# Gate and up products of a transformer trunk's last feed-forward half as block products: seven half-sized products in the place of eight

## The chip, the cores and the metric

The kernel runs on one core of a Trainium2 chip. Its engines are PE (TensorE, matrix products), DVE (VectorE), ACT (ScalarE), POOL (GpSimd) and SP (SyncE, which issues the loads). Each takes its instructions in a fixed order and waits for the others by semaphores. The metric is the device time of one execution in microseconds (us), lower is better.

## The reference

Two layers on 512 latent tokens and 256 context tokens of 1024 channels, in fp32. Each layer is a feed-forward half, a mixer (a convolution module in layer 0, neighbourhood attention in layer 1) and a second feed-forward half. The change touches the last one alone, which works on the 512 latent tokens (`D = 1024`, `F = 2816`):

```
def _swiglu(h, wg, wu, wd):
    return (jax.nn.silu(h @ wg) * (h @ wu)) @ wd

def _ffn_half(s, mod, g, wg, wu, wd):
    shift, scale, gate = mod
    h = _modulate(_rmsnorm(s, g), shift, scale)
    return s + 0.5 * gate * _swiglu(h, wg, wu, wd)
...
    return _rmsnorm(x, final_g)
```

## The kernel before

Channels lie on the partitions, tokens on the free axis; 1024 channels are 8 chunks of 128. fp32 accuracy comes from splitting: every weight tile and every activation is split into a rounded part `hi` (ACT, a copy to fp32r) and a remainder `lo` (DVE, a subtraction `src - hi` of two SBUF operands), and `mm3` makes three matmuls of each product: hi x hi, hi x lo, lo x hi.

The feed-forward half (`ffn`) runs over 22 blocks of 128 hidden columns in `GROUPS` of 5, 5, 6 and 6. For a block it loads a gate and an up tile of 128 x 1024 weights (`load`, three buffers each of `raw`, `whi`, `wlo`), and for the last half of the kernel makes products for two pieces of tokens (`HALVES`: 256 and 256 + 2 columns; the two extra columns hold the products of the shift vector). A block is therefore 2 weights x 2 pieces x 8 chunks x 3 = 96 matmuls. The factor of the norm, `rb`, is applied to the products when DVE reads them out of PSUM (`by_rows`, L289); then come SiLU on ACT (L318), `tu` on DVE (L319) and the split of the hidden tile into `hidh` and `hidl` (L115, L116). After each group, `down` multiplies the group's hidden tiles with `dn` for 8 output chunks `d` and adds to `x` (L296). In the last group the two halves of the tokens (`LATS`) go one after the other, and `finish` normalises and stores the first half while the second is worked on: its column sums are L182, its factor is made by the Newton steps (L166 to L177), spread by L194, and the outputs are multiplied at L852, on POOL for the first half and on DVE for the second.

Before this half stand the attention's output products: 8 units of 24 matmuls of 512 columns (L833 to L835 evict them), and then `scaled_parts` (L225, L226) makes the half's input `h` from `x`. The tiles of `h` take over the buffers of the attention's output (tags `hhi` and `hlo`), chunk by chunk as the last unit has read them.

The order of the instructions on each engine is made by a list scheduler when the program is built; the tile pools' buffers decide what may overlap. PSUM has 8 banks: three of tag `a`, two of `b`, two of `c` and one `st`.

## Time and profile before

| what | us |
|---|---|
| median of 3 runs | 2747.91 (2747.2 to 2749.19) |
| span of the profiled execution | 2745.9 |
| PE busy in it | 2700.0 (98%) |
| DVE, ACT, POOL busy | 1673.2, 822.1, 68.1 |
| last feed-forward half: first product to the end | 2351.3 to 2745.9 |

The span runs from the first to the last instruction in the profile. The profiled execution's own time is not listed apart from its span; the timed executions are 1.3 to 3.3 us longer than that span, and 2.0 us is taken for what lies around it. Busy is the time in which an engine works on at least one instruction; PE overlaps its matmuls, so what a matmul costs is read from the distance of the starts of two that follow each other.

### The profile page before, as it was taken

How to read it: one execution, taken by the hardware profiler on the slowest of the kernel's cores; microseconds unless marked ns; L12 is line 12 of the kernel's file. 1: busy time of each engine (PE TensorE's matmuls, PEld its weight loads, DVE VectorE, ACT ScalarE, POOL GpSimd, SP SyncE). 2: the span in 40 equal slices, each digit the busy share in tenths (PEclk: the TensorE clock that was granted, in tenths of full speed). 3: DMA queues.
4: the chain of work that ended last, by engine and by line, in shares of the span. 5: the costliest groups of instructions: out<-in, count | busy, mean ns of one | idle time of the engine just before them, and what ended most of it. 6: DMA issues, size and time to landing. Idle time of an engine off the chain costs nothing.

```text
span 2745.9 us, 41215 instructions
## 1 busy us (share of the span) xinstructions
PE 2700.0 (98%) x16948; PEld 2353.4 (86%) x16948; DVE 1673.2 (61%) x3048; ACT 822.1 (30%) x1306; POOL 68.1 (2%) x124
## 2 busy tenths in 40 slices
PE   8999999999989999999999999999999999999997
PEld 4888888888869888888888888888888888999997
DVE  5999533357998999833363433433478576544446
ACT  4212221241236212121242221212346455422224
POOL 0000000011020100000000000000000000000001
PEclk9999999999999999999999999999999999999999
DMA  8565212122435565412121212121242121233223
GB/s 297 163 211 175 88 55 71 56 71 78 127 78 178 168 195 177 158 54 70 58 72 50 75 50 67 61 69 61 80 121 62 58 73 46 74 105 95 88 99 112
DMA packets 95101, 277.73 MB, mean 101 GB/s; under 512 B 11329, under 2 KB 25793, under 8 KB 94657
## 3 DMA queue, kind: packets, MB, share of 16 engines
q1 hardware_dynamic: 94336, 273.52, 31.4%
q8 instruction: 133, 2.18, 0.3%
q0 software_dynamic: 576, 1.57, 0.2%
q14 instruction: 56, 0.45, 0.1%
HBM read 269.09 MB, written 4.38 MB: 100 GB/s over the span
## 4 chain that ended last, share of the span: by engine, by line
PE 93%; DVE 3%; ACT 1%; issue 1%; DMA 1%; POOL 0%; SPq 0%; DVEq 0%; POOLq 0%; ACTq 0%
PE a L125 12%; PE a L123 12%; PE a L124 11%; PE c L123 9%; PE c L125 9%; PE c L124 9%; PE b L125 8%; PE b L124 8%; PE b L123 8%; PE st L793 2%; PE b L784 1%; DVE y L514 1%; PE c L532 1%; PE a L759 1%; PE a L760 1%
## 5 line engine op out<-in xcount | busy, mean ns | idle before, releaser
L110 ACT ACTIVATE whi<-raw 128x1024 fp32r<-128x1024 f32 (+2 forms) x376 | 360.0, 960 | 1437.8 <-PE c L124 1046.0
L111 DVE TENSOR_TENSOR wlo<-raw,whi 128x1024 fp32r<-128x1024 f32 (+2 forms) x376 | 411.8, 1098 | 100.1 <-ACT whi L110 98.1
L125 PE MATMUL a<-hhi,wlo 128*128 128x512 f32 (+2 forms) x1264 | 442.2, 350 | 0.4 <-DVE wlo L111 0.4
L124 PE MATMUL a<-hlo,whi 128*128 128x512 f32 (+2 forms) x1264 | 440.3, 348 | 0.0
L123 PE MATMUL a<-hhi,whi 128*128 128x512 f32 (+2 forms) x1264 | 440.3, 349 | 0.0
L123 PE MATMUL c<-hhi,whi 128*128 128x258 f32 (+2 forms) x1456 | 428.6, 295 | 4.3 <-ACT hhi L115 2.1
L125 PE MATMUL c<-hhi,wlo 128*128 128x258 f32 (+2 forms) x1456 | 429.2, 295 | 0.0
L124 PE MATMUL c<-hlo,whi 128*128 128x258 f32 (+2 forms) x1456 | 427.1, 294 | 0.5 <-DVE hlo L116 0.5
L375 DVE SCALAR_TENSOR_TENSOR junk<-mraw,sbc 128x1024 f32<-128x1024 f32 x256 | 312.7, 1221 | 3.8 <-ACT sbc L360 2.0
L123 PEld LDWEIGHTS c<-hhi,whi 128*128 128x128 f32 x1456 | 275.7, 190 | 15.6 <-ACT hhi L115 2.7
L123 PE MATMUL b<-hhi,whi 128*128 128x512 f32 (+2 forms) x800 | 280.3, 350 | 6.0 <-ACT hhi L225 3.4
L124 PEld LDWEIGHTS c<-hlo,whi 128*128 128x128 f32 x1456 | 276.7, 190 | 10.8 <-DVE hlo L116 1.3
L125 PE MATMUL b<-hhi,wlo 128*128 128x512 f32 (+2 forms) x800 | 280.9, 351 | 0.5 <-DVE wlo L111 0.5
L125 PEld LDWEIGHTS c<-hhi,wlo 128*128 128x128 f32 x1456 | 275.1, 189 | 7.1 <-issue 1.0
L124 PE MATMUL b<-hlo,whi 128*128 128x512 f32 (+2 forms) x800 | 280.1, 350 | 0.5 <-DVE hlo L226 0.5
L125 PEld LDWEIGHTS a<-hhi,wlo 128*128 128x128 f32 x1264 | 237.8, 188 | 34.0 <-issue 1.1
L124 PEld LDWEIGHTS a<-hlo,whi 128*128 128x128 f32 x1264 | 238.1, 188 | 32.9 <-issue 0.2
L123 PEld LDWEIGHTS a<-hhi,whi 128*128 128x128 f32 x1264 | 238.0, 188 | 31.3 <-issue 0.8
L123 PEld LDWEIGHTS b<-hhi,whi 128*128 128x128 f32 x800 | 151.0, 189 | 29.6 <-ACT hhi L225 3.6
L124 PEld LDWEIGHTS b<-hlo,whi 128*128 128x128 f32 x800 | 151.0, 189 | 22.8 <-DVE hlo L226 1.0
L125 PEld LDWEIGHTS b<-hhi,wlo 128*128 128x128 f32 x800 | 150.9, 189 | 22.2 <-DVE wlo L111 1.0
L124 PE MATMUL a<-hidl,whi 128*128 128x512 f32 (+1 forms) x431 | 162.7, 377 | 0.0
(202 smaller groups left out, 4169.8 us busy)
## 6 DMA issues: line engine op xcount, KB each, us to landing
raw<-in_gu SPq DMA_DIRECT2D x176, 512.0 KB
mraw<-in_modv SPq DMA_DIRECT2D x128, 512.0 KB
raw<-in_dn SPq DMA_DIRECT2D x80, 384.0 KB
raw<-in_dn SPq DMA_DIRECT2D x64, 320.0 KB
raw<-in_pw SPq DMA_DIRECT2D x24, 512.0 KB
us<-v SPq DMA_DIRECT2D x64, 142.0 KB
mraw<-in_modp SPq DMA_DIRECT2D x16, 512.0 KB
raw<-in_wqk SPq DMA_DIRECT2D x16, 512.0 KB
```

What stands on the lines that cost most here:

```text
L110: nc.scalar.activation(hi[:, :cols], raw[:, :cols], AF.Copy)
L111: nc.vector.tensor_tensor(lo[:, :cols], raw[:, :cols], hi[:, :cols].bitcast(F32), ALU.subtract)
L123: nc.tensor.matmul(po, lhsT=whi[:, s], rhs=ah[:, o:o + n], start=first and i == 0, stop=False)
L124: nc.tensor.matmul(po, lhsT=whi[:, s], rhs=al[:, o:o + n], start=False, stop=False)
L125: nc.tensor.matmul(po, lhsT=wlo[:, s], rhs=ah[:, o:o + n], start=False, stop=last and i == k - 1)
L375: nc.vector.scalar_tensor_tensor(junk, raw, 1.0, sbc[:, s, :], ALU.mult, ALU.mult, accum_out=m[:, s, c:c + 1])
L514: nc.vector.scalar_tensor_tensor(yo, u[:, k:k + n], w, yo, ALU.mult, ALU.add)
L532: nc.tensor.matmul(po[ST * g:ST * g + ST, e:e + PIECE], lhsT=dg[:, 4 * m + g], rhs=t[:, g, 4 * m:4 * m + PIECE], start=m == 0, stop=m == 7)
L759: nc.tensor.matmul(so, lhsT=qq[:, qsl], rhs=kk[:, ks], start=True, stop=False)
L760: nc.tensor.matmul(so, lhsT=ql[:, qsl], rhs=kk[:, ks], start=False, stop=True)
L784: nc.tensor.transpose(pt[:, i * P:(i + 1) * P], p[:, i * P:(i + 1) * P], ident)
L793: nc.tensor.matmul(po[64 * a:64 * a + 64, :P], lhsT=v[:, c0:c0 + 64], rhs=PT[a][:, i * P:(i + 1) * P], start=i == 0, stop=i == 3)
```

## The change

For the last half, the gate and the up weights are taken in pairs of blocks: 256 hidden columns by 1024 channels. With the channels cut into two halves (even and odd chunks), the tokens into two halves of 256 (each with a shift column pair, so 258 columns), and the hidden columns into two blocks, a pair is a 2 x 2 by 2 x 2 block product. `s_unit` makes it of seven products of half the depth (4 chunks, 12 matmuls of 258 columns) instead of eight: 84 matmuls for a unit (gate or up of a pair) in the place of 96. Products 1 to 4 and 5 to 7 are named after the operands that they need:

* `s_prepare` makes sums and differences of the activations once (`tt`, four DVE subtractions for each of 4 steps `j`), and splits all seven operands into the buffers that held `h`; `slots[:4]` hold operands 1, 2, 3, `slots[4:]` operands 5, 6, 7, and `t4` operand 4. The scaling by the modulation is done into `sg` tiles (two buffers) beforehand.
* `s_weights` makes sums and differences of the weights for every unit on POOL: four instructions of 128 x 512, two SBUF operands each, into `s12` and `s34` (one buffer each). Four tiles are split for a unit, of 1024, 1024, 1024 and 512 columns: the raw tile for products 1 and 2, `s12` for 6 and 5, `s34` for 7 and 3, and half of the second raw tile for product 4. They go through the same three `whi` and `wlo` buffers.
* Products 1, 6, 7 and 4 accumulate in one PSUM bank (`a`), 5 and 3 in another (`c`), 2 in a third (`b`). Intermediate states are copied out by ACT (`kept`, L396; L414), and DVE adds them to the banks (L403, L410, L412). The norm's factor is applied afterwards, on SBUF tiles (L967, L974).
* The groups are `PAIRS` of 3, 3, 3 and 2 pairs, that is 6, 6, 6 and 4 blocks, so `down` has 432 matmuls of 512 columns and 192 of 256 instead of 384 and 288.

The rest of the program, up to the last output product of the attention, stands in the same order as before. The diff, cut to its core:

```diff
-TB = T + 2
+SB = 258
+TB = 3 * SB
...
+PAIRS = (3, 3, 3, 2)
...
+    def s_weights(src, pool):
+        raws = []
+        for i in range(2):
+            raw = main.tile([P, 1024], F32, tag="raw", name="raw", bufs=3)
+            nc.sync.dma_start(raw, src[i])
+            raws.append(raw)
+        q = [raws[0][:, :512], raws[0][:, 512:], raws[1][:, 512:], raws[1][:, :512]]
+        s12 = pool.tile([P, 1024], F32, tag="s12", name="s12", bufs=1)
+        s34 = pool.tile([P, 1024], F32, tag="s34", name="s34", bufs=1)
+        s1, s2, s3, s4 = s12[:, 512:], s12[:, :512], s34[:, :512], s34[:, 512:]
+        sums = ((s1, q[2], q[3], ALU.add), (s2, s1, q[0], ALU.subtract), (s3, q[0], q[2], ALU.subtract),
+                (s4, q[1], s2, ALU.subtract))
+        made = {}
+        for t, names in ((raws[0], (1, 2)), (s12, (6, 5)), (s34, (7, 3)), (raws[1], (4,))):
+            if t is s12:
+                for o, a, b, op in sums:
+                    nc.gpsimd.tensor_tensor(o, a, b, op)
+            n = 512 * len(names)
+            hi = main.tile([P, 1024], F32R, tag="whi", name="whi", bufs=3)
+            lo = main.tile([P, 1024], F32R, tag="wlo", name="wlo", bufs=3)
+            split(hi[:, :n], lo[:, :n], t[:, :n])
+            for i, name in enumerate(names):
+                made[name] = (hi, lo, 512 * i)
+        return made
+    def s_unit(src, hs, pool, row):
+        w = row.shape[3]
+        made = s_weights(src, pool)
+        def product(name, p, first):
+            hi, lo, o = made[name]
+            for j in range(4):
+                k = slice(o + j * P, o + j * P + P)
+                ah, al = hs[name][j]
+                for i, (a, b) in enumerate(((hi, ah), (hi, al), (lo, ah))):
+                    nc.tensor.matmul(p, lhsT=a[:, k], rhs=b, start=first and j == 0 and i == 0,
+                                     stop=j == 3 and i == 2, skip_group_check=True)
+        def kept(p):
+            t = pool.tile([P, w], F32, tag="kept", name="kept", bufs=4)
+            nc.scalar.activation(t, p, AF.Copy)
+            return t
+        x, y = bank("a")[:, :w], bank("b")[:, :w]
+        product(1, x, True)
+        a = kept(x)
+        product(2, y, True)
+        nc.vector.tensor_tensor(row[:, 0, 0], y, a, ALU.add)
+        product(6, x, False)
+        b = kept(x)
+        z = bank("c")[:, :w]
+        product(5, z, True)
+        d = kept(z)
+        product(7, x, False)
+        nc.vector.tensor_tensor(row[:, 1, 1], x, d, ALU.add)
+        product(3, z, False)
+        nc.vector.tensor_tensor(row[:, 0, 1], z, b, ALU.add)
+        product(4, x, False)
+        nc.scalar.activation(row[:, 1, 0], x, AF.Copy)
+    def s_prepare(j, hs, sx, tt, A, B):
+        for r in range(2):
+            c = 2 * j + r
+            nc.scalar.activation(sx[:, r, :, :256], xl[c].rearrange("p (b n) -> p b n", b=2), AF.Identity,
+                                 scale=A[:, 0, c:c + 1])
+            nc.gpsimd.tensor_copy(sx[:, r, :, 256:], B[:, 0, c:c + 1].rearrange("p (a b) -> p a b", a=1).broadcast_to([P, 2, 2]))
+        nc.vector.tensor_tensor(tt[:, 0], sx[:, 0, 1], sx[:, 0, 0], ALU.subtract)
+        nc.vector.tensor_tensor(tt[:, 1], sx[:, 1, 1], tt[:, 0], ALU.subtract)
+        nc.vector.tensor_tensor(tt[:, 2], sx[:, 1, 1], sx[:, 0, 1], ALU.subtract)
+        nc.vector.tensor_tensor(tt[:, 3], sx[:, 1, 0], tt[:, 1], ALU.subtract)
+        for names, src in (((1,), sx[:, 0, :1]), ((2, 3), sx[:, 1]), ((5, 6, 7), tt[:, :3]), ((4,), tt[:, 3:])):
+            to = hs[names][j]
+            split(to[0], to[1], src)
...
-        h = new_h()
...
-        for d in range(NC):
-            scaled_parts(h, d, (LAT,), derv[1, 7], mods[1, 6])
+    with tc.tile_pool(name="ffn3", bufs=1) as hid:
+        slots = new_h()
+        t4 = [hid.tile([P, 4, SB], F32R, name=f"t4{i}") for i in range(2)]
+        hs = {}
+        for names, of in (((1, 2, 3), slots[:4]), ((5, 6, 7), slots[4:])):
+            for i, n in enumerate(names):
+                hs[n] = [tuple(t[:, i * SB:(i + 1) * SB] for t in of[j]) for j in range(4)]
+        hs[4] = [tuple(t[:, j] for t in t4) for j in range(4)]
+        spans = {}
+        for names in ((1,), (2, 3), (5, 6, 7)):
+            of = slots[:4] if names[0] < 5 else slots[4:]
+            o = SB if names[0] == 2 else 0
+            spans[names] = [tuple(t[:, o:o + len(names) * SB].rearrange("p (a n) -> p a n", n=SB) for t in of[j])
+                            for j in range(4)]
+        spans[(4,)] = [tuple(t[:, j:j + 1] for t in t4) for j in range(4)]
+        def rows(tag):
+            return hid.tile([P, 2, 2, SB], F32, tag=tag, name=tag, bufs=2)
+        for j in range(4):
+            s_prepare(j, spans, rows("sg"), rows("tu").rearrange("p a b n -> p (a b) n"), derv[1, 7], mods[1, 6])
         rms_rows((LAT,), True)
...
-        ffn(3, h, hid, HALVES, (1, 8), nothing, finish)
+        rows_rb = rb[:, :TL].rearrange("p (b n) -> p b n", b=2)
+        pair = 0
+        for gi, gn in enumerate(PAIRS):
+            last = gi == len(PAIRS) - 1
+            hids = []
+            f0 = 2 * pair
+            for _ in range(gn):
+                sg, tu = rows("sg"), rows("tu")
+                s_unit(gs[pair, 0], hs, hid, sg)
+                for r in range(2):
+                    so = sg[:, r, :, :256]
+                    nc.vector.tensor_tensor(so, so, rows_rb, ALU.mult)
+                    nc.scalar.activation(so, so, AF.Silu, bias=sg[:, r, 0, 256:257])
+                s_unit(gs[pair, 1], hs, hid, tu)
+                for r in range(2):
+                    to = tu[:, r, :, :256]
+                    hh = hid.tile([P, TL], F32R, tag="hidh", name="hidh", bufs=7)
+                    hl = hid.tile([P, TL], F32R, tag="hidl", name="hidl", bufs=7)
+                    nc.vector.tensor_tensor(to, to, rows_rb, ALU.mult)
+                    nc.vector.scalar_tensor_tensor(to, to, tu[:, r, 0, 256:257], sg[:, r, :, :256], ALU.add, ALU.mult)
+                    split(hh.rearrange("p (b n) -> p b n", b=2), hl.rearrange("p (b n) -> p b n", b=2), to)
+                    hids.append((hh, hl))
+                pair += 1
+            for st in LATS if last else (LAT,):
+                for d in range(NC):
+                    n = 2 * gn * P
+                    w = load(dn[3, d, :, f0 * P:f0 * P + n], n)
+                    down(d, w, hids, st, derv[1, 8], last)
+                if last:
+                    finish(st)
...
+def _quarters(w):
+    k, m = w.shape
+    t = w.reshape(k // 256, 2, P, m // 256, 2, P).transpose(3, 4, 2, 1, 0, 5)
+    t = np.stack([t[:, 0], t[:, 1, :, ::-1]], axis=1)
+    return t.reshape(m // 256, 2, P, k)```

Three places of the order on the engines, in which the names are `raw` loaded weights, `s12` and `s34` the POOL's sums, `whi` and `wlo` split weights, `sg` the gate's and `tu` the up's tile of a pair, `kept` a copied PSUM state, and `a`, `b`, `c` PSUM banks. The first place is the middle of a group. On DVE, before, a block's instructions stand like this:

```order
L289 TENSOR_TENSOR sg_22106<-a_22006,rb_84 128x256
L289 TENSOR_TENSOR tu_22109<-b_22031,rb_84 128x256
L289 TENSOR_TENSOR sg_22106<-a_22056,rb_84 128x256
L282 COPY bcol_22112<-a_22056 128x2
L111 TENSOR_TENSOR wlo_22129<-raw_22126,whi_22128 128x1024
L289 TENSOR_TENSOR tu_22109<-a_22081,rb_84 128x256
L282 COPY bcol_22114<-a_22081 128x2
L319 SCALAR_TENSOR_TENSOR tu_22109<-tu_22109,bcol_22114,sg_22106 128x512
L111 TENSOR_TENSOR wlo_22251<-raw_22248,whi_22250 128x1024
L116 TENSOR_TENSOR hidl_22005<-tu_22109,hidh_22004 128x512
```

On DVE in the changed kernel, a gate unit's stretch there, in which the hidden tiles of the pair before are finished (`tu_21939`, `hidl`) among the weight splits of this unit and the first of the next one (`raw_22331`):

```order
L403 TENSOR_TENSOR sg_22202<-b_22231,kept_22244 128x258
L118 TENSOR_TENSOR wlo_22223<-s34_22209,whi_22222 128x1024
L118 TENSOR_TENSOR hidl_22191<-tu_21939,hidh_22190 128x512
L974 TENSOR_TENSOR tu_21939<-tu_21939,rb_84 128x2x256
L118 TENSOR_TENSOR wlo_22227<-raw_22206,whi_22226 128x512
L975 SCALAR_TENSOR_TENSOR tu_21939<-tu_21939,sg_21938 128x2x256
L118 TENSOR_TENSOR wlo_22338<-raw_22331,whi_22337 128x1024
L410 TENSOR_TENSOR sg_22202<-a_22230,kept_22286 128x258
L118 TENSOR_TENSOR hidl_22197<-tu_21939,hidh_22196 128x512
L412 TENSOR_TENSOR sg_22202<-c_22273,kept_22271 128x258
L118 TENSOR_TENSOR wlo_22346<-s12_22335,whi_22345 128x1024
L967 TENSOR_TENSOR sg_22202<-sg_22202,rb_84 128x2x256
```

A unit has seven to nine DVE instructions with two SBUF operands here, and three that read PSUM; before, a block of two weights had four such with two SBUF operands. The second place is the same stretch on ACT, in the up unit that follows:

```order
L396 ACTIVATE kept_22371<-a_22357 128x258
L117 ACTIVATE whi_22349<-s34_22336 128x1024
L968 ACTIVATE sg_22202<-sg_22202 128x2x256
L117 ACTIVATE whi_22353<-raw_22333 128x512
L414 ACTIVATE sg_22202<-a_22230 128x258
L396 ACTIVATE kept_22398<-a_22357 128x258
L968 ACTIVATE sg_22202<-sg_22202 128x2x256
L117 ACTIVATE whi_22474<-raw_22468 128x1024
```

The first split of the next unit, `whi_22474`, stands behind the second SiLU of the gate (the second L968), which needs DVE's L967 on what L414 copied. The third place is the head of a group on PE, where product 6 of a unit ends (`whi_21954`), the first matmuls of the next unit's products 1 and 2 follow (`whi_22073`), and then product 7 begins (`whi_21958`):

```order
L391 MATMUL a_21966<-hhi7_20840,whi_21954 128x258
L391 MATMUL a_21966<-hlo7_20841,whi_21954 128x258
L391 MATMUL a_21966<-hhi7_20840,wlo_21955 128x258
L391 MATMUL a_22093<-hhi0_20826,whi_22073 128x258
L391 MATMUL a_22093<-hlo0_20827,whi_22073 128x258
L391 MATMUL b_22094<-hhi0_20826,whi_22073 128x258
L391 MATMUL b_22094<-hlo0_20827,whi_22073 128x258
L391 MATMUL a_21966<-hhi4_20834,whi_21958 128x258
```

`whi_22073` takes over the buffer of `whi_21954`. In the other units product 7 stands ahead of these four matmuls. On PE the order in a unit, from then on, is: 2 matmuls of product 5, product 6, the other 10 of product 5, product 7, two each of the next unit's products 1 and 2, product 3, the other ten each of the next 1 and 2, and product 4 at their end or 4 matmuls ahead of it.

## Rows read from the trace of the kernel before

**Rows 1.** The page's busy times, share of the span and instructions of each engine.

```profile
PE 2700.0 (98%) x16948; PEld 2353.4 (86%) x16948; DVE 1673.2 (61%) x3048; ACT 822.1 (30%) x1306; POOL 68.1 (2%) x124
```

**Rows 2.** Windows (us from the span's start) of the last half.

```profile
core 0: us, PE busy (x) PEld busy (x) DVE busy (x) ACT busy (x) POOL busy (x), PEclk, DMA share, GB/s
2351.00:2400.00 49.00, 46.76 (x386) 45.66 (x384) 27.05 (x67) 18.90 (x32) 0.00 (x0) 1.00 0.22 68
```

**Rows 3.** Groups by form, 2340 to 2746 us: busy us, mean ns, idle before.

```profile
L124 PE MATMUL a<-hlo,whi 128*128 128x258 f32 x216 | 61.1, 283 | 0.0
...
L111 DVE TENSOR_TENSOR wlo<-raw,whi 128x1024 fp32r<-128x1024 f32 x44 | 53.8, 1223 | 14.9 <-ACT whi L110 13.9
...
L319 DVE SCALAR_TENSOR_TENSOR tu<-tu,bcol,sg 128x512 f32<-128x512 f32 x22 | 16.5, 752 | 2.9 <-ACT whi L110 0.5 <-ACT sg L318 0.4
L318 ACT ACTIVATE sg<-sg,bcol 128x512 f32<-128x512 f32 x22 | 15.6, 709 | 0.3 <-DVE bcol L282 0.3
...
L116 DVE TENSOR_TENSOR hidl<-tu,hidh 128x512 fp32r<-128x512 f32 x22 | 15.1, 686 | 0.0
...
L289 DVE TENSOR_TENSOR tu<-a,rb 128x256 f32<-128x256 f32 x27 | 11.4, 424 | 36.9 <-PE a L125 36.9
```

**Rows 4.** Timeline of PE into the last half: start, duration, instruction, idle before.

```profile
2345.76 0.40 PE L123 MATMUL a<-hhi,whi 128*128 128x512 f32 x1
...
2351.10 0.40 PE L125 MATMUL a<-hhi,wlo 128*128 128x512 f32 x1
...
2359.31 0.29 PE L124 MATMUL a<-hlo,whi 128*128 128x258 f32 x1
...
2361.12 0.28 PE L124 MATMUL a<-hlo,whi 128*128 128x258 f32 x1
...
2364.03 0.28 PE L123 MATMUL a<-hhi,whi 128*128 128x256 f32 x1
...
2366.38 0.28 PE L125 MATMUL a<-hhi,wlo 128*128 128x256 f32 x1
2367.76 1.10 PE L194 MATMUL st<-t,ones 128*128 128x512 f32 x2 [1.09 <-DVE t L188]
2370.00 0.39 PE L123 MATMUL b<-hhi,whi 128*128 128x256 f32 x1 [1.15 <-DVE sg L289]
```

**Rows 5.** Timeline of ACT and DVE, same stretch.

```profile
2354.41 0.76 ACT L833 ACTIVATE t<-a,dv,mod 128x512 f32<-128x512 f32 x1
...
2363.29 2.01 ACT L110 ACTIVATE whi<-raw 128x1024 fp32r<-128x1024 f32 x2 [5.40 <-PE b L124]
...
2365.59 1.22 DVE L111 TENSOR_TENSOR wlo<-raw,whi 128x1024 fp32r<-128x1024 f32 x1
2366.73 0.16 DVE L173 SCALAR_TENSOR_TENSOR nwt<-nwt 128x4 f32<-128x4 f32 x1
```

**Rows 6.** Timeline of DVE and POOL where both work.

```profile
40.74 0.80 POOL L209 TENSOR_TENSOR acc<-acc,t 128x256 f32<-128x256 f32 x1
40.87 0.95 DVE L226 SCALAR_TENSOR_TENSOR hlo<-xc,dv,hhi 128x256 fp32r<-128x256 f32 x1
...
2724.69 0.42 DVE L209 TENSOR_TENSOR acc<-acc,t 128x256 f32<-128x256 f32 x1
...
2725.99 5.11 POOL L852 TENSOR_TENSOR out<-out,rb 128x1024 f32<-128x1024 f32 x2 [3.65 <-ACT rb L218]
2726.42 2.44 DVE L209 TENSOR_TENSOR acc<-acc,t 128x256 f32<-128x256 f32 x1
2728.78 0.47 DVE L296 SCALAR_TENSOR_TENSOR x<-b,dv,x 128x256 f32<-128x256 f32 x1
```

**Rows 7.** One POOL line's instructions: ns min/median/max.

```profile
L520 POOL TENSOR_TENSOR dg<-eye,parts x12: 1906/2024/8445, 596.8 to 799.0; 128x1024 f32<-128x1024 f32 x12
```

**Rows 8.** Timeline of PE at the kernel's end.

```profile
2730.00 0.28 PE L125 MATMUL b<-hidh,wlo 128*128 128x256 f32 x1
2734.16 1.02 PE L182 MATMUL st<-ones,acc 128*128 128x1 f32 x4 [3.88 <-DVE acc L209]
```

More of the change, by code (lines that the diff above doesn't have):

```diff
@@ L55, in tile_trunk @@
 @with_exitstack
-def tile_trunk(ctx: ExitStack, tc, xin, cb, cs, par, modp, modv, gu, dn, pw1, pw2, wqk, wv, wo, bv, rpb, out):
+def tile_trunk(ctx: ExitStack, tc, xin, cb, cs, par, modp, modv, gu, gs, dn, pw1, pw2, wqk, wv, wo, bv, rpb, out):
     nc = tc.nc
@@ L835, in tile_trunk @@
             square_in(d, LAT)
-        for d in range(NC):
-            scaled_parts(h, d, (LAT,), derv[1, 7], mods[1, 6])
+    with tc.tile_pool(name="ffn3", bufs=1) as hid:
[17 more added lines that the diff above has]
+            s_prepare(j, spans, rows("sg"), rows("tu").rearrange("p a b n -> p (a b) n"), derv[1, 7], mods[1, 6])
         rms_rows((LAT,), True)
-    with tc.tile_pool(name="ffn3", bufs=1) as hid:
         def finish(st):
@@ L905, in _layout @@
     gate, up, down = (i[k].reshape(4, *i[k].shape[2:]) for k in ("ffn_w_gate", "ffn_w_up", "ffn_w_down"))
-    g["gu"] = np.stack([np.stack([_tiles(gate[k]), _tiles(up[k])], axis=1) for k in range(4)])
+    g["gu"] = np.stack([np.stack([_tiles(gate[k]), _tiles(up[k])], axis=1) for k in range(3)])
+    g["gs"] = np.stack([_quarters(gate[3]), _quarters(up[3])], axis=1)
     g["dn"] = np.stack([_tiles(down[k]) for k in range(4)])
@@ L918, in _layout @@
     return {k: np.ascontiguousarray(v) for k, v in g.items()}
-_INS = ["xin", "cb", "cs", "par", "modp", "modv", "gu", "dn", "pw1", "pw2", "wqk", "wv", "wo", "bv", "rpb"]
+_INS = ["xin", "cb", "cs", "par", "modp", "modv", "gu", "gs", "dn", "pw1", "pw2", "wqk", "wv", "wo", "bv", "rpb"]
 def kernel(**inputs):
```

1 line of the change is left out of this document (added).

## The prediction

> **What bounds the kernel now.** The page comes first: PE is busy for 98% of the span [rows 1], so the question is what PE waits for and what one of its matmuls costs. The windows show the last half alone: PE at the full clock (PEclk 1.00, that is 2.4 GHz) and busy but for 2.2 us of the first 49, DVE about half busy, POOL idle [rows 2]. The timeline gives the cost of a matmul as the distance of two starts: 512 columns 5.34 us over 23 steps, 0.2322; 258 columns 1.81 over 15, 0.1207; 256 columns 2.35 over 20, 0.1175 [rows 4]. The recorded 283 ns of such a matmul [rows 3] overlap. So PE time in this half goes by columns, and fewer matmuls are worth their full price as long as the other engines deliver. The reader should also see one hole: PE stands still from the start at 2366.38 to 2370.00, about 3.6 us, while the norm's factor is made and DVE can't free the PSUM banks without it [rows 4].
>
> **What is removed on PE.** Gate and up before: 22 blocks x 96, half of 256 and half of 258 columns, 1056 x 0.1175 + 1056 x 0.1207 = 251.5 us. After: 22 units x 84 = 1848 x 0.1207 = 223.1. The down products: 48 more of 512 columns (+11.1) and 96 fewer of 256 (-11.3). Together **-28.6 us**. If 258-column slices that begin at other offsets cost more, this shrinks; no row shows that, and I add nothing for it.
>
> **What is added, engine by engine.** DVE instructions overlap by some 0.08 us: a split of 1024 columns is recorded with 1.22 and followed by the next start after 1.14 [rows 5]. With 0.08 off the means [rows 3], a split of 512 or a product with `rb` is 0.61, the line like L319 0.66, and an addition from PSUM 0.34 (nearest row: L289, 424 ns). Per pair DVE then has 6 x 1.14 + 2 x 0.61 of weight splits, 6 x 0.34, and 4 x 0.61 + 2 x 0.66 + 2 x 0.61 on the tiles: about 15.1 us, of which 13.0 have two SBUF operands. PE needs 168 x 0.1207 = 20.3 us for a pair. DVE alone would do.
>
> POOL's eight sums a pair decide. No row has one of 128 x 512; L209 with 256 columns takes 0.80 and L520 with 1024 takes 1.9 at least [rows 6, 7], so one takes about 1.2 us. What they do to DVE is in [rows 6]: L209 on DVE, 0.42 us elsewhere, took 2.44 while POOL's L852 (2.56 each) ran, 2.02 longer; L226 with 256 columns took 0.95 beside a POOL instruction of 256, against the 0.47 of L296, which has the same form and size, 0.48 longer. L296 reads PSUM, and took its 0.47 although POOL ran beside it. So a POOL instruction holds up DVE instructions with two SBUF operands for most of its length: 0.48 at 256, 2.02 at 1024, hence about 0.97 us at 512. The Trainium skill has this as a rule (SBUF — State Buffer, section "SBUF: two separate sides"): VectorE instructions with two SBUF inputs and GpSimd instructions share one port pair, which the first to start locks for its whole instruction. The rows agree on the lock, but the hold that they show is shorter than the instruction.
>
> So 8 x 0.97 = 7.8 us of POOL and 13.0 of DVE exclude each other: 20.8 of 20.3 us. That isn't hopeless over a group, since the last unit of a group has no sums beside it and the first has some made during the down products. But the splits have dates. I follow one unit; 0 is the start of its product 5.
>
> *Gate unit.* The buffer for its `s34` split is freed by product 4 of the unit before, 0.5 us before 0; ACT (1.0 us a split [rows 5]) is done at 0.55. POOL's second sum holds the port until 1.2, the low part is done at 2.3. Then in DVE's order `hidl` to 2.9, POOL's third sum to 3.9, L974 to 4.5, the fourth sum to 5.5, the split for product 4 to 6.1, L975 to 6.7, and the next unit's first low part to 7.9. PE wants it after products 5, 6, 7, four matmuls and product 3 (52 x 0.1207) at 6.3: **1.6 late**. Without the sums it would be there at 5.3, **0 late**.
>
> *Up unit.* The same split is done on ACT at 1.0 and on DVE at 2.5; the split for product 4 at 3.1, POOL's third sum 4.1, L967 4.7, then the second SiLU on ACT (0.63 after overlap) 5.3, and only then the next unit's first high part, 6.3. PE wants it at 4.35: **1.95 late**; without the sums 5.1, **0.75 late**.
>
> *Head of a group.* Product 7 stands behind matmuls that need a split whose buffer product 6 frees: one split on ACT, **1.1**.
>
> There are 11 gate and 11 up units. The 4 up units that end a group have no following unit; in the 4 gate units that begin one, two splits are made before, and I take half, 0.8. Three heads (the first group's order is another): 3.3. In full: 3.3 + 4 x 0.8 + 7 x 1.6 + 7 x 1.95 = 31.4 us. With the sums costing nothing: 3.3 + 7 x 0.75 = 8.6. POOL got the port within a DVE instruction or two nearly always (L520's median 2.0 is near its minimum of 1.9, though one took 8.4 [rows 7]), so I take a value near the upper end: **+29**.
>
> **The start.** Before, ACT and DVE scale and split chunk by chunk, and PE has work from 2351.3 on; its loss is the 3.6 us hole. After, ACT first holds one 1024-column split and the eviction of the last attention unit (at 2354.4 before [rows 5]), and steps 2 and 3 need the two `sg` buffers of steps 0 and 1. A step costs DVE 4 differences at 0.34 and 1806 columns of splits (0.34 + 0.6 + 0.87 + 0.34), 3.5 us. Adding these up in DVE's order, with the split of `s34` (1.14), the last `x` and the squares, step 3 is ready at about 2362.7. PE has products 1, 2, 5 and 6 until then (48 x 0.1207 = 5.8 us from 2351.3), so it ends them at 2363.6 instead of 2357.1: 6.5 lost. L194 now stands in PE's order among the next products and waits some 1.2 for DVE and takes 1.1; four sums of POOL in the way cost DVE about 1.5. Together 10.3, **+6.7** net; bounds +1 (steps go by PE's other work) to +11 (each of eight sums holds DVE here).
>
> **The end.** Before, PE stops at 2730.3 and its last column sums wait until 2734.16 for DVE, held up by L852 on POOL [rows 6, 8]. After, the second half of the tokens takes PE 96 x 0.1175 = 11.3 us instead of 144 x 0.1175 = 16.9, so L852 falls on the last Newton steps and multiplications instead: it moves the hold, and saves or costs up to 4. Steps of 12 matmuls (1.4 us) are about what DVE needs for theirs (0.61 + 0.39 + 0.34) and what a load allows, +1. I take **+0.5**, -3 to +4.
>
> **The sum.** -28.6 + 29 + 6.7 + 0.5 = +7.6 us on a span of 2745.9, 2753.5; with 2.0 around it **2755 us**, against a median of 2747.91. PE's clock is left at full: the rows show PEclk 1.00 over the window with the 3.6 us hole [rows 2], and the new waits are of that length or shorter.
>
> **Rivals.**
> *The sums slip in* (faster). POOL takes DVE's waits for ACT and PE, and the splits are on time; the waits are those worked out without sums. For it: DVE has 5 us a pair without work, and L296 shows that PSUM instructions go on beside POOL. Against it: in the gate unit DVE has none of those waits between 1.2 and 6.7. -28.6 + 8.6 + 6.7 + 0.5 = -12.8: 2735. It decides from the point where stalls in the units are under 16 us.
> *Half of it* (no change). POOL is sometimes held off by a chain of DVE instructions, as the 8.4 us of L520 show, and comes in at the PSUM additions: 20 us of stalls, 2746.
> *The hold is the whole instruction* (slower). If a sum keeps the port for its recorded 1.2 us instead of 0.97, two sums in each of 14 units add 14 x 2 x 0.23 = 6.4: 2762. The 0.48 beside a record of 0.80 speak against it. This is what the rule of the Trainium skill's SBUF page (same section) would give.
>
> **Chances.** About 0.2% (5.5 us) is what a measurement of this kernel can tell from no change. My forecast has 0.38, with a range of its own of 2750 to 2766; the longer hold 0.07; half 0.27; sums that slip in 0.28. So faster 0.28, no change 0.27, slower 0.45. The range must reach into the faster case's middle, and above it takes in the longer hold with the start's upper bound: 2734 to 2770.
>
> **What would show it right or wrong.** PE: 1848 matmuls with starts 0.1207 apart, and idle time of some 20 to 30 us spread over the units, ended by ACT's `whi` or DVE's `wlo`, least in the last unit of a group. A pair in the middle of a group should take about 23.8 us instead of 20.3. DVE's splits and tile products beside POOL should be 0.5 to 1 us longer than 1.22 and 0.69 in many places, its PSUM additions not. POOL's sums should take 1.2 to 2 us. If splits keep their length and pairs take 21, the sums slip in. The hole before the first SiLU should be gone, and one of 6 us should stand in the first 12. Wrong from the ground up I'd be if the 258-column matmuls keep another distance, or if PE's clock falls at the start.

## The result and the profile after

The changed kernel takes **2780.05 us** in the median of 4 executions (2774.3 to 2784.5), against 2747.84 (2747.2 to 2749.2): 1.0115 times as long, 95% interval 1.0101 to 1.0130. The prediction had the sign (slower) but not the size: 2755, range 2734 to 2770. The profiled execution, the longest of the four, has a span of 2782.7 us, 36.8 more than before.

The windows of the changed kernel answer to [rows 2]. The granted clock (PEclk) is below 1.00 in the stretches in which the units of a group run, and PE is busy for only 42 to 44 of 50 us there; where down products fill the stretch (2450 to 2500) it is as before:

```profile
core 0: us, PE busy (x) PEld busy (x) DVE busy (x) ACT busy (x) POOL busy (x), PEclk, DMA share, GB/s
2351.00:2400.00 49.00, 41.53 (x262) 37.97 (x261) 40.59 (x60) 26.62 (x44) 19.81 (x16) 0.83 0.14 44
2450.00:2500.00 50.00, 48.48 (x307) 43.04 (x306) 32.59 (x35) 19.84 (x30) 19.02 (x13) 1.00 0.31 100
2500.00:2550.00 50.00, 42.20 (x310) 40.94 (x310) 39.25 (x44) 21.99 (x37) 18.96 (x12) 0.93 0.25 76
```

From the distances of PE's matmul starts, in each trace from 2351.2 to the last down product, with 0.119 us taken for 258 columns, 0.2322 for 512 and 0.1165 for 256: distances over 0.5 us above these count as waits; the smaller excesses are parted by the granted clock at their place, 0.50 (that is 1.2 GHz) or full.

| us | before | changed | difference |
|---|---|---|---|
| work | 372.1 | 344.5 | -27.7 |
| waits | 2.9 | 39.7 | +36.8 |
| smaller excesses at half clock | 0 | 17.9 | +17.9 |
| smaller excesses at full clock | 3.4 | 10.2 | +6.8 |
| from the last down product to the end | 15.6 | 18.6 | +3.0 |
| sum | | | +36.8 |

(Before, a further 3.9 us of wait lies behind the last down product [rows 8] and is counted in the last row, in the changed kernel 6.5.) Of the 17.9 us at half clock, 5.9 fall into the first 24 us and 12.0 into the units. So the saving on PE came as forecast; waits and a slower PE took more than twice as much back. The waits of PE, by what ended them:

```profile
engine line waited for: us in total, times, longest us
PE a L391 <- DVE wlo L118: 19.5, 8, 3.6
PE a L391 <- ACT whi L117: 9.0, 9, 2.0
```

The groups of DVE instructions by form answer to [rows 3] (busy us, mean ns, idle before). Those with two SBUF operands are longer than they were, 1.45 and 1.54 us for 1.22, 1.45 for 0.69; the additions out of PSUM (L403) are not:

```profile
L118 DVE TENSOR_TENSOR wlo<-s,whi 128x1024 fp32r<-128x1024 f32 x44 | 63.8, 1449 | 9.8 <-ACT whi L117 7.0 <-PE a L391 2.5
L118 DVE TENSOR_TENSOR wlo<-raw,whi 128x1024 fp32r<-128x1024 f32 x22 | 34.0, 1544 | 9.2 <-ACT whi L117 8.7
L118 DVE TENSOR_TENSOR wlo<-raw,whi 128x512 fp32r<-128x512 f32 x22 | 31.8, 1447 | 1.4 <-ACT whi L117 1.3
...
L403 DVE TENSOR_TENSOR sg<-b,kept 128x258 f32<-128x258 f32 x11 | 4.7, 426 | 7.7 <-PE b L391 6.6 <-ACT whi L117 1.0
```

One wait in the middle of a group shows how it comes about. These are rows of the timeline, engine by engine (start, duration, instruction, idle before): the gate unit whose split of `s34` opens at 2497.68.

```profile
2497.43 0.28 PE L391 MATMUL a<-t,wlo 128*128 128x258 f32 x1
...
2497.68 1.06 ACT L117 ACTIVATE whi<-s 128x1024 fp32r<-128x1024 f32 x1 [1.69 <-PE a L391]
...
2498.78 2.37 DVE L118 TENSOR_TENSOR wlo<-s,whi 128x1024 fp32r<-128x1024 f32 x1
2501.06 1.80 DVE L118 TENSOR_TENSOR hidl<-tu,hidh 128x512 fp32r<-128x512 f32 x1
2502.78 1.80 DVE L974 TENSOR_TENSOR tu<-tu,rb 128x512 f32<-128x512 f32 x1
2504.50 1.78 DVE L118 TENSOR_TENSOR wlo<-raw,whi 128x512 fp32r<-128x512 f32 x1
2506.20 0.74 DVE L975 SCALAR_TENSOR_TENSOR tu<-tu,sg 128x512 f32<-128x512 f32 x1
2506.87 1.21 DVE L118 TENSOR_TENSOR wlo<-raw,whi 128x1024 fp32r<-128x1024 f32 x1
...
2498.74 1.31 POOL L371 TENSOR_TENSOR s<-raw 128x512 f32<-128x512 f32 x1 [5.79 <-DVE sg L403]
2500.13 2.18 POOL L371 TENSOR_TENSOR s<-s,raw 128x512 f32<-128x512 f32 x1
2502.25 1.78 POOL L371 TENSOR_TENSOR s<-raw 128x512 f32<-128x512 f32 x1
2503.99 1.74 POOL L371 TENSOR_TENSOR s<-raw,s 128x512 f32<-128x512 f32 x1
...
2504.27 0.28 PE L391 MATMUL c<-hhi,wlo 128*128 128x258 f32 x1
2508.13 0.39 PE L391 MATMUL a<-hhi,wlo 128*128 128x258 f32 x1 [3.58 <-DVE wlo L118]
```

Read it from the top. PE's last matmul of product 4 frees a weight buffer; ACT splits, then DVE runs six instructions one behind the other until 2508.08, and PE takes the last one's result at 2508.13. DVE never idles in these 9.3 us. But the first four take 1.09 to 1.15 us longer than alone (1.22, 0.68, 0.68, 0.69), and in each of them POOL works on one of its sums: POOL and DVE take turns. 4 x 1.12 = 4.5 of the 9.3 us are the time lost to POOL's sums.

Behind this wait PE runs at half clock. The windows behind it, and around the 1.73 us wait that follows at 2519.78:

```profile
2509.00:2512.00 3.00, 3.00 (x16) 3.00 (x15) 2.08 (x4) 0.39 (x1) 0.00 (x0) 0.50 0.50 175
2508.13:2513.58 5.45, 5.45 (x32) 5.45 (x33) 3.58 (x7) 2.17 (x4) 1.31 (x1) 0.69 0.42 152
2518.00:2521.00 3.00, 1.27 (x11) 1.22 (x11) 1.26 (x3) 1.94 (x3) 1.16 (x1) 1.00 0.31 127
```

The second of these windows holds 32 matmuls, up to the first one behind the next product 4. A wait of nearly the same kind, of 2.63 us, ends at 2427.90, and behind it the clock stays up: the corresponding 32 matmuls take 3.97 us instead of 5.45.

```profile
2427.90 0.39 PE L391 MATMUL a<-hhi,wlo 128*128 128x258 f32 x1 [2.63 <-DVE wlo L118]
...
2427.90:2431.87 3.97, 3.97 (x33) 3.97 (x33) 3.53 (x7) 2.21 (x4) 0.00 (x0) 1.00 0.54 171
```

The start of the half, where before the clock was 1.00 [rows 2]: rows of the windows, and of the timelines of PE, DVE and POOL.

```profile
2351.00:2362.00 11.00, 6.16 (x29) 4.28 (x28) 11.00 (x14) 8.64 (x15) 7.37 (x8) 0.84 0.00 0
2362.00:2372.00 10.00, 9.36 (x39) 8.57 (x40) 9.34 (x27) 4.23 (x9) 0.00 (x0) 0.50 0.01 2
...
2362.55 0.58 PE L391 MATMUL a<-hlo,whi 128*128 128x258 f32 x1 [3.47 <-DVE hlo L118]
...
2358.96 1.78 DVE L914 TENSOR_TENSOR x<-x,t 128x512 f32<-128x512 f32 x1
2360.67 1.50 DVE L423 TENSOR_TENSOR tu<-sg 128x258 f32<-128x258 f32 x1
...
2358.78 1.42 POOL L371 TENSOR_TENSOR s<-raw 128x512 f32<-128x512 f32 x1 [2.18 <-DVE wlo L118]
2360.15 1.73 POOL L371 TENSOR_TENSOR s<-raw,s 128x512 f32<-128x512 f32 x1
```

PE is busy for 6.2 of the first 11 us; the next 10 run at 1.2 GHz. Here too two sums stand in DVE's way: L914 takes 1.78 instead of 0.68, L423 1.50 instead of 0.42.

And the end, which answers to [rows 6, 8]: the wait before the last column sums has grown from 3.88 to 6.46, because POOL's two output multiplications meet the last additions of squares, as before [rows 6], and four of these now take 6.11 us (0.42 each alone).

```profile
2764.83 6.11 DVE L211 TENSOR_TENSOR acc<-acc,t 128x256 f32<-128x256 f32 x4
...
2765.31 4.82 POOL L951 TENSOR_TENSOR out<-out,rb 128x1024 f32<-128x1024 f32 x2 [2.85 <-ACT rb L220]
...
2770.99 1.02 PE L184 MATMUL st<-ones,acc 128*128 128x1 f32 x4 [6.46 <-DVE acc L211]
```

### The profile page after: what moved, and what is told of

Its sections match the earlier page's. It is cut to its first block, busy times and chain, and to the rows that moved or that the text cites. A ratio compares the mean times of both kernels' runs of the same rounds, so it can differ in the third digit from the quotient of the medians.

```text
span 2782.7 us, 40958 instructions
## 1 busy us (share of the span) xinstructions
PE 2700.1 (97%) x16636; PEld 2339.2 (84%) x16636; DVE 1789.1 (64%) x3078; ACT 887.8 (32%) x1438; POOL 210.2 (8%) x220
## 4 chain that ended last, share of the span: by engine, by line
PE 89%; DVE 6%; issue 1%; ACT 1%; DMA 1%; POOL 0%; SPq 0%; DVEq 0%; ACTq 0%; POOLq 0%
PE a L127 10%; PE a L125 10%; PE a L126 9%; PE c L125 9%; PE c L127 9%; PE c L126 9%; PE b L127 6%; PE b L125 6%; PE b L126 6%; PE a L391 4%; PE st L874 2%; PE c L391 1%; DVE wlo L118 1%; PE b L865 1%; PE b L391 1%
## 5 line engine op out<-in xcount | busy, mean ns | idle before, releaser
L112 ACT ACTIVATE whi<-raw 128x1024 fp32r<-128x1024 f32 (+3 forms) x332 | 311.5, 942 | 1246.2 <-PE c L126 1045.3
L125 PE MATMUL c<-hhi,whi 128*128 128x258 f32 (+2 forms) x1456 | 428.5, 295 | 4.3 <-ACT hhi L117 2.1
L113 DVE TENSOR_TENSOR wlo<-raw,whi 128x1024 fp32r<-128x1024 f32 (+3 forms) x332 | 355.5, 1073 | 89.3 <-ACT whi L112 88.2
L127 PE MATMUL a<-hhi,wlo 128*128 128x512 f32 (+1 forms) x832 | 321.0, 386 | 0.4 <-DVE wlo L113 0.4
L125 PE MATMUL a<-hhi,whi 128*128 128x512 f32 (+1 forms) x832 | 319.1, 384 | 0.0
L126 PE MATMUL a<-hlo,whi 128*128 128x512 f32 (+1 forms) x832 | 318.8, 383 | 0.0
L125 PEld LDWEIGHTS c<-hhi,whi 128*128 128x128 f32 x1456 | 275.7, 190 | 15.6 <-ACT hhi L117 2.7
L125 PE MATMUL b<-hhi,whi 128*128 128x512 f32 (+1 forms) x528 | 204.0, 386 | 4.9 <-ACT hhi L227 3.4
L127 PE MATMUL b<-hhi,wlo 128*128 128x512 f32 (+1 forms) x528 | 204.8, 388 | 0.5 <-DVE wlo L113 0.5
L126 PE MATMUL b<-hlo,whi 128*128 128x512 f32 (+1 forms) x528 | 203.6, 386 | 0.8 <-DVE hlo L228 0.8
L125 PEld LDWEIGHTS a<-hhi,whi 128*128 128x128 f32 x832 | 156.4, 188 | 31.2 <-issue 0.8
L125 PE MATMUL a<-hidh,whi 128*128 128x512 f32 (+1 forms) x432 | 165.1, 383 | 0.9 <-ACT hidh L117 0.4
L127 PE MATMUL a<-hidh,wlo 128*128 128x512 f32 (+1 forms) x432 | 164.0, 380 | 0.2 <-DVE wlo L113 0.2
L125 PE MATMUL c<-hidh,whi 128*128 128x256 f32 x528 | 149.3, 283 | 0.0
```

The source lines that it names most:

```text
L112: nc.scalar.activation(hi[:, :cols], raw[:, :cols], AF.Copy)
L113: nc.vector.tensor_tensor(lo[:, :cols], raw[:, :cols], hi[:, :cols].bitcast(F32), ALU.subtract)
L125: nc.tensor.matmul(po, lhsT=whi[:, s], rhs=ah[:, o:o + n], start=first and i == 0, stop=False)
L126: nc.tensor.matmul(po, lhsT=whi[:, s], rhs=al[:, o:o + n], start=False, stop=False)
L127: nc.tensor.matmul(po, lhsT=wlo[:, s], rhs=ah[:, o:o + n], start=False, stop=last and i == k - 1)
```

## Experiments

The theories in turn: **A**, POOL's sums hold up DVE's instructions with two SBUF operands, and that makes the waits. **B**, the added work of ACT and DVE is late by its order or amount, whoever makes the sums. **C**, loads come late. **D** and **E** came with the later runs.

One thing has to be known for all of them: the list scheduler makes the order of the engines anew for every version. The two runs without sums keep the changed kernel's order on PE, DVE and ACT, and the one with four load buffers nearly so; with the sums on DVE, with matmuls filled in place and with a tile of its own for product 4 the order changes too, and what such a run gains belongs to the edit and the new order together.

### Without the sums, and with POOL only writing

```diff
-                    nc.gpsimd.tensor_tensor(o, a, b, op)
+                    nc.gpsimd.memset(o, 0.01)
```

> The four sums of weight quarters on POOL are replaced by POOL writing a constant into the same tiles, at the same places of the order (this leaves the sums out, so the products are not the reference's). POOL stays busy, but it no longer reads two SBUF operands, and the sums no longer wait for the loads. Theory A (a POOL sum holds up DVE's instructions with two SBUF operands, about 1.1 us each, and the waits so made drop PE's clock): if a write of a constant holds nothing, PE's waits in the units fall from some 30 us to under 10, the clock stays at 1.00 outside the first 25 us, and the time is 2735 to 2745; if any POOL instruction holds DVE, it stays at 2770 or more with DVE splits still 1.4 to 1.5 us. Theory B (the order and amount of the added ACT and DVE work makes the splits late, whoever makes the sums): 2770 to 2785 with splits at 1.22 us.

The other run takes the line out and fills `s12` and `s34` once, ahead of the units.

> No sums at all: the splits of the second and third part of a unit's weights read two tiles that are filled once (this leaves the sums of the weights out, so the products are not the reference's). Theory A: as forecast without sums, 8.6 us of waits in the units, of which none is long enough to drop the clock; -28 of PE work, +9 of waits, about +12 at the start and +3 at the end: 2740 to 2748. Theory B: waits of 2.5 us and more remain in every second unit and the time is 2765 or more. Theory C (loads come late because the three load buffers are held by the sums): also fast here, but then the run with sums on DVE, which holds them as long, stays slow.

Measured: 2736.91 and **2737.17 us** (ratios 0.9956 and 0.9959). Both are theory A's, the second a little better than expected. The splits of `s` are back at their length (ns, minimum/median/maximum; the first fence is the run in which POOL writes, the second the run without sums), and the stretch of a pair in the second run is filled by PE at full clock:

```profile
L118 DVE TENSOR_TENSOR wlo<-s,whi x40: 1214/1224/1228, 2381.6 to 2680.2; 128x1024 fp32r<-128x1024 f32 x40
```

```profile
L118 DVE TENSOR_TENSOR wlo<-s,whi x40: 1214/1225/1226, 2382.5 to 2681.1; 128x1024 fp32r<-128x1024 f32 x40
...
2482.00:2502.30 20.30, 20.30 (x172) 20.30 (x171) 15.81 (x23) 12.52 (x21) 0.00 (x0) 1.00 0.31 105
```

So the sums cost 2780.05 - 2737.17 = 43 us. And it isn't POOL's being busy: POOL that writes a constant holds nothing. The Trainium skill says this (SBUF — State Buffer, section "Who interferes with whom"): a VectorE instruction with two SBUF inputs contends with a GpSimd instruction that reads SBUF, not with one that only writes it. The run in which POOL writes agrees: the splits kept 1.22 us.

Both runs have the changed kernel's order, so nothing but the sums differs. By the distances of PE's starts, the 47.8 us between the two profiled spans (2782.7 and 2734.9) are 26.4 of waits in the units (31.2 against 4.8), 12.0 of half clock there (against none), 3.9 of waits at the start, and 5.5 in small pieces. So the chain runs from the sums to the waits, and from the waits to the clock.

### The sums on DVE

```diff
-                    nc.gpsimd.tensor_tensor(o, a, b, op)
+                    nc.vector.tensor_tensor(o, a, b, op)
```

> The four sums of weight quarters of a unit run on DVE instead of POOL, all else as changed. Theory A (hold): a sum then costs DVE about 0.61 us instead of the 1.13 that the POOL sum takes from it, 2.1 us less in front of each next split, so the waits of 2.6 to 3.7 us fall to 0.5 to 1.6 and those of 0.9 to 1.9 to nothing, the clock stays up, and the time is 2745 to 2760. Theory B (amount of DVE work): DVE has 20 us of work in a pair of 20.3 us of PE, and its waits for ACT and PE come on top, so it is 2780 to 2800.

Measured: **2746.09 us**, ratio 0.9991 (0.9982 to 1.0001). A sum takes DVE 0.68 us instead of the 1.12 that it lost to POOL's. DVE has more instructions, B expected it slower, and it is 34 us faster. That B falls rests on the two runs before, which keep the order; here the order is another too.

```profile
L371 DVE TENSOR_TENSOR s<-raw x42: 680/684/695, 2348.1 to 2681.4; 128x512 f32<-128x512 f32 x42
```

### Four load buffers

In the changed kernel the load of a unit's second quarters is issued at 2494.09, when a split has freed one of three buffers, and its last packet lands at 2498.25; POOL's first sum begins at 2498.74, behind the end of DVE's L403, which its row names. So all four sums stand ahead of the next split, where the forecast had three. Is that loop the cause?

```diff
-            raw = main.tile([P, 1024], F32, tag="raw", name="raw", bufs=3)
+            raw = pool.tile([P, 1024], F32, tag="rs", name="rs", bufs=4)
```

> As changed, sums on POOL, but the quarters are loaded into four buffers of their own instead of the three that all weight loads share (to make room, the hidden rows have 6 buffers instead of 7 and the output tile one instead of two). Theory A (the hold alone): every sum still takes 1.1 us from DVE, four of them stand in front of the next unit's split, and the time stays at 2770 to 2785. Theory C (a loop through the loads: a unit's second load is issued only when the split of the unit before has freed its buffer, lands 4.1 to 4.5 us later, then four sums of 1.3 to 2.2 us and two splits, 14 us a unit): with the fourth buffer the loads are early, the loop is cut, a mid pair takes 21 to 24 us instead of 25.5 to 27.6, and the time is 2745 to 2762.

Measured: 2778.2 us. C falls as the main cause. The first sum of the unit that corresponds does start ahead of the split, at 2491.32 (split at 2493.39), and three sums are left in front of PE; its wait is still 2.31 us, and the distance of two such waits 25.3 instead of 26.4 us. New waits of 1.7 us for the first down weights of three groups take about 5 us back; whether the smaller hidden buffers cause them was not tried.

```profile
2501.32 0.39 PE L391 MATMUL a<-hhi,wlo 128*128 128x258 f32 x1 [2.31 <-DVE wlo L118]
```

With the sums on DVE the loads give nothing either:

> Sums on DVE and the quarters in four buffers of their own (hidden rows 6 buffers, output tile one). Without POOL the units show hardly any wait for weights but 1.2 us at two places a group, so the loads have little to give: 2743 to 2747. If the loads still delay the first group and the heads, 2738 to 2742.

Measured: 2746.99, as without it (2746.09).

### What half clock costs in the units

```diff
+        for i in range(fill):
+            if i == 0:
+                warm = pst()
+            nc.tensor.matmul(warm[:, :w], lhsT=hs[1][0][0][:, :P], rhs=hs[1][0][0], start=True, stop=True)
```

> As changed, with 18 matmuls of 258 columns into an unused PSUM bank ahead of each up unit but the first (2.2 us of PE work where PE now waits 2.5 to 3.7 us; their product is not used). If the waits are what drops PE's clock, the clock stays at 1.00 through these ten units, the waits shrink by the 2.2 us that the added work fills, and the kernel loses the 1.6 to 2 us of half clock that follow each of them: 16 to 20 us less than the changed kernel, 2760 to 2766. If the clock falls for another reason (the form of the matmuls, their rate over the whole half), the granted clock keeps its dips and the time is 2775 or more; if the added matmuls only come on top, up to 2800.

Measured: 2786.74. The edit did not do what it was meant to: these matmuls depend on nothing of their unit, and the list scheduler moved all 180 forward, to between 2377 and 2486.5 us, that is into the first group, its down products and the head of the second. There 180 x 0.12 = 21.6 us of added work made the kernel only 6.7 us longer.

But the run answers the question all the same, in its second group. From product 4 to product 4, that stretch has the same instructions in the same order on PE, DVE, ACT and POOL as the changed kernel's, and no half clock. The first fence is the run, the second the changed kernel:

```profile
2492.75:2552.64 59.89, 52.77 (x419) 51.09 (x417) 49.89 (x55) 29.91 (x49) 23.99 (x16) 1.00 0.26 81
...
2513.90 0.39 PE L395 MATMUL a<-hhi,wlo 128*128 128x258 f32 x1 [2.47 <-DVE wlo L118]
...
2513.90:2517.86 3.96, 3.96 (x33) 3.96 (x34) 3.54 (x7) 2.21 (x4) 0.00 (x0) 1.00 0.64 215
```

```profile
2485.82:2549.81 63.99, 55.71 (x419) 54.05 (x418) 50.71 (x55) 29.94 (x49) 26.10 (x16) 0.95 0.25 76
```

It takes 4.1 us less. Of these, 1.1 are the first wait (2.47 instead of 3.58). The other 3.0 are two stretches of half clock: from a wait's end to the start behind the next product 4, the 32 matmuls take 3.96 us instead of 5.45. That is 1.5 us a stretch, and it is on the path, since product 4 opens the chain of the next unit, and the next units take as long as in the changed kernel (11.53 and 9.98 us against 11.59 and 9.96).

The second attempt repeats the first matmul of the unit itself, which can't move away:

```diff
+        for i in range(fill):
+            nc.tensor.matmul(x, lhsT=made[1][0][:, :P], rhs=hs[1][0][0], start=True, stop=False, skip_group_check=True)
         product(1, x, True)
```

> As changed, but the first matmul of each up unit but the first is made 19 times over in its place (2.2 us of PE work; the result is the same). If half clock behind the waits is paid on top of the waits, the kernel gains some 15 to 20 us, 2760 to 2766. If the loop of loads, sums and splits sets the pace, the filling stands in PE's idle time: the dips of the granted clock in the windows of the second to fourth group go away, PE's waits shrink by about what is filled in, and the time still stays at 2775 to 2788, because PE was waiting for DVE either way.

Measured: 2785.88. The dip behind the wait is gone:

```profile
2508.90:2534.40 25.50, 22.68 (x184) 22.27 (x184) 22.69 (x23) 12.05 (x21) 14.74 (x8) 1.00 0.24 79
```

Yet from one such wait's end to the next it takes 25.5 us instead of 26.4 (2508.13 to 2534.51). This does not measure the clock: the scheduler also moved product 4, which now stands 3 matmuls behind the wait's end instead of 20. And the added matmuls cost elsewhere: from the last product 4 of a group to the first of the next it takes 2 us longer (46.1 instead of 44.1), and the last unit of each group 3.3 us longer (13.3 instead of 10.0). So the time does not say that the half clock was free.

The Trainium skill (TensorE: Matmul & The Clock Gate, section "HAM oscillation — how this bites in real kernels") counts the clock's loss as extra wall time on top of the waits. These traces agree, with 1.5 us for a stretch in the units.

### The chain's beginning

What is left: PE ends product 4, ACT splits, DVE works off its list with POOL in between, PE goes on; this chain is longer than the work that PE has left meanwhile. Theory **D** says that it must begin earlier; **E** that DVE and POOL together have too much to do.

```diff
+            if names == (4,):
+                hi = pool.tile([P, 512], F32R, tag="qhi", name="qhi", bufs=1)
+                lo = pool.tile([P, 512], F32R, tag="qlo", name="qlo", bufs=1)
```

> As changed, sums on POOL, but the split for product 4 has a high and a low tile of its own (512 columns), so the split of s34 no longer waits for product 4 of the unit before. Theory D (a serial loop: PE's products up to product 4, then ACT's split, then DVE's chain with three or four holds, 15 to 16 us from one wait's end to the next): the chain starts 3 us or more earlier, the waits of 2.6 to 3.7 us fall below 1, a mid pair takes 22 to 24 us, and the time is 2750 to 2762. Theory E (the amount: DVE's own work and eight holds of 1.13, 15.1 + 9.0 = 24.1 us a pair, and idle stretches of DVE that the order leaves): a mid pair stays at 25 us or more and the time at 2768 to 2782.

Measured: **2752.95 us**, 27 less than the changed kernel (ratio to before 1.0019, 1.0010 to 1.0028). The time is D's; mid pairs take 24.1 to 24.6 us, a little more than D's 22 to 24. POOL still makes every sum and DVE is still held (2.37), but ahead of PE's need: PE's longest wait for a low part is now 0.9 us, its longest in the units 1.5 (for `kept`), and the clock is 1.00 in all six windows of 50 us from 2400 to 2700.

```profile
2485.74 2.37 DVE L118 TENSOR_TENSOR wlo<-s,whi 128x1024 fp32r<-128x1024 f32 x1
...
2490.08 2.00 DVE L118 TENSOR_TENSOR wlo<-raw,whi 128x1024 fp32r<-128x1024 f32 x1
2492.00 1.78 DVE L118 TENSOR_TENSOR qlo<-raw,qhi 128x512 fp32r<-128x512 f32 x1
...
PE a L395 <- ACT kept L400: 4.0, 6, 1.5
PE c L395 <- DVE wlo L118: 1.7, 2, 0.9
...
2500.00:2550.00 50.00, 47.66 (x304) 42.33 (x303) 39.07 (x45) 20.59 (x35) 12.39 (x7) 1.00 0.31 96
```

Two things differ in this stretch. The split of `s34` starts 0.9 us ahead of product 4's end (2486.63) instead of 1.2 behind it. And DVE's order is another: the split for product 4 (`qlo`) stands behind the next unit's low part, where it stood in front of it, so the chain up to that low part takes 6.3 us (2485.74 to 2492.08) instead of 9.3. No run parts the earlier beginning from the new order. The amount of work, E's cause, is the same while the time falls by 27 us, so the amount alone isn't the cause.

### The start, the end, and a version that is faster than both

With the sums on DVE the clock still falls in the first 20 us. Matmuls into an unused bank, behind the first three of the preparing steps:

```diff
+            if j < 3:
+                warm = pst()
+                for _ in range(12):
+                    nc.tensor.matmul(warm[:, :SB], lhsT=hs[1][j][0][:, :P], rhs=hs[1][j][0], start=True, stop=True)
```

> Sums on DVE (2746.1 us), with 12 matmuls of 258 columns into an unused bank behind each of the first three steps that prepare the activations (1.45 us each, product not used). If PE's starving during these steps is what brings the clock down to half from 2356 to 2366 us, the clock stays at 1.00 there and 4 to 6 us are gained: 2740 to 2742. If DVE's work sets the pace of the start whatever the clock, it is 2745 to 2748; if the added matmuls come on top, 2750.

Measured: 2742.75 (ratio 0.9979, 0.9970 to 0.9988), 3.3 less, which is under the 4 to 6 expected; a short stretch at half clock is left (2362.62 to 2366.03). The windows of 2351 to 2362 us, without and with the filling:

```profile
2351.00:2362.00 11.00, 8.24 (x36) 6.37 (x36) 11.00 (x22) 7.72 (x13) 1.46 (x2) 0.70 0.00 0
```

```profile
2351.00:2362.00 11.00, 9.81 (x74) 9.08 (x74) 11.00 (x22) 8.43 (x15) 1.85 (x4) 1.00 0.01 1
```

With the sums on POOL the same filling:

> Sums on POOL and product 4 in a tile of its own (2752.95 us), with 12 matmuls of 258 columns behind each of the first three preparing steps. If half clock at the start is on the path, as with the sums on DVE, where filling gave 3.3 us, it gives 3 to 7 us here: 2746 to 2750. If POOL's sums set the pace of the start by holding DVE's preparing steps, the clock comes back but the time stays at 2751 to 2755.

Measured: 2752.18 (2748.6 to 2756.7), against 2752.95 (2751.7 to 2755.8). The clock came back, the time can't be told from the one without. The gain expected from the clock did not show; that the sums' pace hides it fits, but the scatter leaves it open.

Then both edits with the sums on DVE:

> Sums on DVE, the start filled with matmuls (2742.75 us so far), and the split for product 4 in a tile of its own. Theory D: the two waits of 1.19 us at the head of each group, where a split waits for a buffer that PE frees, go away or shrink, 7 x 1.19 = 8 us at most: 2735 to 2740. Theory E: DVE, with 20 us of work in a pair of 20.3 us of PE, makes other waits in their place: 2741 to 2746.

Measured: **2731.51 us** (ratio 0.9940), 11.2 less, more than the 8 us bound: the small waits under 0.5 us that the 1.19 us figure left out went too. PE now waits nowhere in the units. Last, the end:

```diff
-            eng = nc.vector if end else nc.gpsimd
+            eng = nc.vector
```

> The kernel with sums on DVE, filled start and own tile for product 4 (2731.5 us), with the two multiplications of the first half of the output made on DVE instead of POOL. If these two hold up the last additions of squares (2.59 and 2.38 us where 0.42 is usual, 4.1 us on the path of the end), two DVE instructions of about 1.2 us in their place make the end 1.5 to 4 us shorter: tail from PE's last down product to the end 15 to 17 us instead of 19, 2727.5 to 2730. If the tail is set by other work: 2731 to 2733.

Measured: **2729.48 us** (ratio 0.9932, 0.9918 to 0.9945), the fastest version. The two multiplications take DVE 2.36 us together, and the additions behind them are short again:

```profile
2712.17 2.36 DVE L959 TENSOR_TENSOR out<-out,rb 128x1024 f32<-128x1024 f32 x2
2714.45 0.95 DVE L211 TENSOR_TENSOR acc<-acc,t 128x256 f32<-128x256 f32 x2
```

## Why the prediction was off

The measured span is 29.2 us above the forecast one (2782.7 against 2753.5). By the table, 17.9 of these are half clock, 6.8 smaller excesses at full clock, 2.5 the end, 1.1 waits (36.8 against 29 + 6.7) and 0.9 PE's work.

* **"PE's clock is left at full"**: this is the step that failed. Half clock was put at nothing, because the hole of 3.6 us before had PEclk 1.00 and the new waits would be of that length or shorter. But two matmuls of L194 stand in that hole, and behind the new waits the clock did fall: 17.9 us are lost by it, 5.9 at the start and 12.0 in the units. The prediction itself had named a fall at the start as a sign of being wrong from the ground up. In the units a stretch costs 1.5 us that PE doesn't win back, as the group with the same order and full clock shows; at the start, with the sums on DVE, filling gave 3.3 us.
* **What is removed on PE**: right. -28.6 forecast, -27.7 by the distances (in the changed trace these include six matmuls of the attention, 1.4 us, that before lie ahead of 2351.2); 258 columns keep their 0.12 us behind every offset.
* **The mechanism of the stalls**: right. The sums hold DVE, PSUM additions aren't held, and the waits are ended by `wlo` in the gate units and by `whi` in the up units.
* **The sum of the stalls**: right by luck. PE's waits in the units are 28.5 us (19.5 + 9.0) against +29, but by terms that were off both ways: the seven gate units in the middle wait 18.8 us instead of 11.2, the seven up units 6.6 instead of 13.65, the four first gate units not at all instead of 3.2; only the heads are as forecast (3.1 against 3.3).
* **The gate unit's chain**: mis-sized. From the end of product 4 to PE's next low part it was put at 8.4 us and takes 10.6 (2497.55 to 2508.13); with these 2.2 us more the forecast wait of 1.6 would be 3.8, and 3.58 is measured. A hold was put at 0.97 us between rows of 256 and 1024 elements and is 1.09 to 1.15 (the rival with the longer hold was nearer in this, and too low as a whole). And three sums were put into DVE's path, where there are four.
* **The price of the sums**: 29 - 8.6 = 20.4 us forecast, 43 measured. In waits of the units it is 26.4; the greatest part of what was missing is the half clock that these waits bring, 12.0, and 3.9 are waits at the start.
* **The kernel without sums**: 2735 forecast, 2737 measured, and this too is right only in sum. Its waits in the units are 3.1 us instead of 8.6, while half clock at the start takes 6.3 instead of nothing, and the end +3.0 instead of +0.5.
* **The start**: forecast +6.7. The waits of the first 12 us are 6.0 (6.5 forecast), and 5.9 us of half clock come on top. The sums' part was put at 1.5 us and is larger: two sums alone took 2.2 us from DVE in the stretch shown.
* **The end**: +0.5 forecast, within -3 to +4; +3.0 measured. The forecast had L951 move to the last Newton steps; it stayed on the last additions of squares, and the wait behind them grew. Making the two multiplications on DVE gave 2 us.

So the direction came from the right mechanism, the sum of the waits by luck, and the size was lost in what the waits do to PE's clock.

What stays open: why one wait of some 2.5 us is followed by half clock and another isn't; what the smaller excesses at full clock are; and how the 27 us of the tile divide between the earlier beginning of the chain and the new order.

## What to carry to other kernels

When an added operation makes a buffer late, follow the chain from the product that frees the buffer, through every engine, to the product that waits, and count each hold and each hand-over in it: here 2.2 us were missing in a chain of 10.6. Then price PE's clock behind the waits as a term of its own, from windows right behind a wait: 1.5 us a stretch here, 12 in all. A small buffer of its own for the tile that opens the chain is worth a try: 4 KB per partition gave 27 us here, together with the order that came with it. An elementwise operation on SBUF that is taken from DVE to POOL to relieve it can cost DVE more (1.12 us) than doing it itself (0.68).
